# A diagonal state-space mixer worked through in batches of two group pairs

## The chip, the cores and the metric

The kernel runs on one core of a Trainium2 chip. The metric is the device time of one execution in microseconds (us), the median over runs. Times inside the execution come from one profiled execution and count from the start of its span. PE is the matmul engine, PEld its weight load, DVE the vector engine, ACT the scalar engine, POOL and SP the other two; SP issues nearly all DMA transfers.

## The reference

The program is one inference step of a two-layer streaming encoder on 1024 prompt positions and 64 sample positions, width 1024, all in fp32. Layer A mixes tokens with windowed attention, layer B with a complex-diagonal state-space model (S5); behind each mixer stands a gated convolutional FFN. The change lies in layer B's mixer alone. What it computes:

```
# 64 groups of 16 channels, a complex state of 64 numbers per group
x_t = B_bar u_t                        # per group, (64 x 16) complex
h_t = lambda_bar * h_(t-1) + x_t       # complex, elementwise, over positions
y_t = Re(C h_t) + d * u_t
z   = gelu(y)
ag  = z @ w_glu + b_glu
out = ag[:, :1024] * sigmoid(ag[:, 1024:])
```

## The kernel before

Activations lie with channels on partitions and the 1088 positions in three blocks of 384, 384 and 320 columns. Every large product is made of three fp32r products, of a high and a low half of both operands (`mm3`, L179); `load_unit` (L161) loads a 128 x 1024 piece of weight (tile `raw`, two buffers) and splits it into `whl` on ACT (L175) and DVE (L176). The program is attention, FFN 0, the state-space mixer `ssm`, its GLU, FFN 1.

The mixer. Eight positions form one column, so the scan runs over 137 columns (128 of the prompt, one empty, 8 of the sample). Two groups share the 128 partitions as a *pair* `q`, so there are 32 pairs. FFN 0 leaves the parameters of each pair in DRAM (`prm`, 1044 numbers per partition): input, direct and output matrices and a table of cosines and sines of the state's angle per column. Rotating by that angle makes the complex recurrence two real ones (real and imaginary part, `c` = 0, 1) with the decay `rho` that one DVE scan instruction (L979) runs over 2 x 138 columns. For each pair, `batch(q)` does

1. `ssm_pm`: load of the parameters (L926, SP) into `pm`, one of six `big` buffers; ACT copies the sines with a minus sign (L928) and writes the mask times rho (L929) beside them;
2. four input products on PE (L969) of `U`, the pair's input, into one of six PSUM banks; DVE multiplies by cosines and sines (L974, L975, the second reading the product's two halves in swapped order), adds (L976); POOL puts the sample's start state in (L977); then a `yield`;
3. DVE's scan (L979), two products to rotate back (L981, L982), ACT's copies of the last states (L985); a `yield`;
4. on PE a direct product of `U` (L990) and the state products (L995) into two PSUM banks, two ACT copies into `ys` (L999). After every fourth pair `ys` holds one tile of 128 channels with positions spread over partitions: it is written to DRAM (`yd`, L1002, ACT's queue), read back in the other arrangement (`yf`, L1007, SP), and ACT takes the gelu (`z`, L1012) and splits it into `zh` (L1019) and, with DVE, `zl` (L1020).

`staged` starts one pair a round and in each round advances the newest live pair first. `U` comes in four quarters of eight pairs (`ssm_load`, two transfers each from `hd`), and DVE multiplies each half quarter by the inverse norm `rs` (L919) as the load is written in the program. Within an engine the instructions run in a fixed order, which the builder's scheduler chose from readiness in its own timeline; SP's transfers stand in one queue.

The GLU (`tile_`, L1028) starts with the products of channel tiles 0 to 6 for its first 128 outputs, for the three blocks one after another, before it needs channel tile 7 (L1040, L1042).

Of the kernel before, what the change touches and what calls it, by code (L numbers as in the profile page):

```python
# [20 lines left out]
BLK = [(0, 384), (384, 384), (768, 320)]  # L21
# [9 lines left out]
NC_ = 137  # L31
NPR = 32

OW, OKT, OC, OCO, OSI, PRM = 0, 256, 512, 768, 906, 1044


class Core:
# [88 lines left out]
        return self.ps.tile([P, 512], F32, name=name, tag=f"sm{i}", bufs=1)  # L126

    @staticmethod
    def staged(units, beside=()):
# [779 lines left out]
    def ssm_load(self, q):  # L909

        nc = self.nc
        u = self.yp.tile([P, 16, NC_], F32, name="U", tag="ypB" if q == 2 else "ypA", bufs=1 if q == 2 else 2)
        for k in range(2):
            uk = u[:, 8 * k:8 * k + 8]
            self.last_u = nc.sync.dma_start(uk, self.hd[(2 * q + k) * P:(2 * q + k) * P + P].rearrange("(g j) s c -> (j s) g c", j=16))
            if k == 0:
                self.first_u = self.last_u
            for x, y in ((0, 2), (2, 8)) if (q, k) == (0, 0) else ((0, 8),):
                nc.vector.tensor_mul(uk[:, x:y], uk[:, x:y], self.rs[:, None, :].to_broadcast([P, y - x, NC_]))  # L919
        return u  # L920

    def ssm_pm(self, q):

        nc = self.nc
        pm = self.big([P, PRM + 414], "pm", F32)
        got = nc.sync.dma_start(pm[:, :PRM], self.prm[:, q])  # L926
        rd = pm[:, PRM + 138:].rearrange("p (c k) -> p c k", c=2)
        self.order(nc.scalar.activation(pm[:, PRM:PRM + 138], pm[:, OSI:PRM], AF.Copy, scale=-1.0), self.last_rs)  # L928
        self.order(nc.scalar.activation(rd, self.mask[:, None, :].to_broadcast([P, 2, 138]), AF.Copy, scale=self.rho[:, q:q + 1]), self.last_rs)  # L929
        return pm, pm[:, PRM + 138:], got  # L930

    def ssm(self, after):
        nc, tc, a = self.nc, self.tc, self.a
        off = PPO
        yd = self.dram.tile([D, 8, NC_], F32, name="yd")
        zh, zl = [None] * 3, [None] * 3
        with tc.tile_pool(name="ss", bufs=1) as sp:
            us = [self.ssm_load(0)]
            self.order(self.hw[1], self.first_u)
            self.order(self.hw[2], self.last_u)  # L940
            us.append(self.ssm_load(1))
            self.order(self.spill(), self.last_u)
            us.append(self.ssm_load(2))
# [5 lines left out]
            self.mask = sp.tile([P, 138], F32, name="mask")  # L949
            nc.gpsimd.memset(self.mask, 1.0)  # L950
            nc.gpsimd.memset(self.mask[:, 0:1], 0.0)
            nc.gpsimd.memset(self.mask[:, 129:130], 0.0)
            ROWS = (slice(0, 64), slice(64, 128))
            got, out = {}, {}

            def batch(q):
                if q == 8:
                    us.append(self.ssm_load(3))
                pm, rd, got[q] = self.ssm_pm(q)
                if q == 31:  # L960
                    self.wsrc.pop(0)
                    self.load_ahead(AHEAD)
                cos = pm[:, None, OCO:OSI].to_broadcast([P, 2, 138])
                sin = pm[:, OSI:OSI + 276].rearrange("p (c k) -> p c k", c=2)
                p1 = self.mm_ps("p1")[:, 0:2 * NC_].rearrange("p (c k) -> p c k", c=2)
                for c in range(2):
                    for e, r in enumerate(ROWS):
                        o = OW + P * c + 64 * e
                        nc.tensor.matmul(p1[r, c], pm[:, o:o + 64], U(2 * q + e), start=True, stop=True)  # L969

                wk = sp.tile([P, 3, 2, 138], F32, name="wk", bufs=5)
                A, t, G = (wk[:, i] for i in range(3))
                nc.gpsimd.memset(A[:, :, 0:1], 0.0)
                nc.vector.tensor_mul(A[:, :, 1:], cos[:, :, 1:], p1)  # L974
                nc.vector.tensor_mul(t[:, :, 1:], sin[:, :, 1:], self.from_last(p1))  # L975
                nc.vector.tensor_add(A[:, :, 1:], A[:, :, 1:], t[:, :, 1:])  # L976
                nc.gpsimd.tensor_copy(A[:, :, 129:130], h0[:, q, :, None])  # L977
                yield
                nc.vector.tensor_tensor_scan(G.rearrange("p c k -> p (c k)"), rd, A.rearrange("p c k -> p (c k)"), 0.0, ALU.mult, ALU.add)  # L979
                gc, gs = t, A  # L980
                nc.vector.tensor_mul(gc, G, cos)  # L981
                nc.vector.tensor_mul(self.from_last(gs), G, sin)  # L982
                for o, g_ in enumerate((gc, gs)):
                    x = g_[:, :, 128:138]
                    nc.scalar.copy(fin[:, o, q], bass.AP(tensor=x.tensor, offset=x.offset, ap=[x.ap[0], [138, 2], [9, 2]]))  # L985
                yield
                p3 = [self.mm_ps("p3")[:, :NC_] for _ in range(2)]
                for e in range(2):
                    o = OKT + P * e
                    nc.tensor.matmul(p3[e], pm[:, o:o + P], U(2 * q + e), start=True, stop=False)  # L990
                for c in range(2):
                    for g_ in (gc, gs):
                        for e, r in enumerate(ROWS):
                            o = OC + P * c
                            nc.tensor.matmul(p3[e], pm[r, o:o + P], g_[r, c, 0:NC_], start=False, stop=c == 1 and g_ is gs)  # L995
                if q % 4 == 0:
                    ys[0] = self.t4([P, 8, NC_], "ys")
                for e in range(2):
                    out[q] = nc.scalar.activation(ys[0][:, 2 * (q % 4) + e], p3[e], AF.Copy)  # L999
                if q % 4 == 3:  # L1000
                    kt = q // 4
                    nc.scalar.dma_start(yd[kt * P:kt * P + P].rearrange("(g i) t c -> (i t) g c", i=16), ys[0])  # L1002

                    for _ in range(min(6, 29 - q)):
                        yield
                    yf = self.t4([P, 8, NC_], "yf")
                    x = nc.sync.dma_start(yf, yd[kt * P:kt * P + P])  # L1007
                    if q < 28:
                        self.order(x, got[min(q + 8, 31)])
# [3 lines left out]
                    if q < 28:  # L1013
                        self.order(x, out[min(q + 5, max(out))])
                    nc.scalar.activation(z[:, SEQ:].rearrange("p (c t) -> p c t", t=8), yv[:, 129:137], AF.Gelu_apprx_tanh)
                    for b, (t0, n) in enumerate(BLK):
                        if kt == 0:
                            zh[b], zl[b] = self.bt(self.blk, b, "zh", F32R), self.bt(self.blk, b, "zl", F32R)
                        nc.scalar.activation(zh[b][:, kt], z[:, t0:t0 + n], AF.Copy)  # L1019
                        nc.vector.tensor_sub(zl[b][:, kt], z[:, t0:t0 + n], zh[b][:, kt].bitcast(F32))  # L1020
            self.staged([batch(q) for q in range(32)])
# [190 lines left out]
```

## Time and profile before

| | |
|---|---|
| runs | median 2365.73 us (2362.16 to 2365.94, 3 runs) |
| the profiled execution | 2358.86 us, its span 2357.1 us |
| PE busy | 2261.0 us (96%), weight loads 2190.1 us (93%) |
| DVE busy | 1469.9 us (62%) |
| ACT busy | 894.6 us (38%) |
| POOL busy | 278.9 us (12%) |
| granted TensorE clock, mean | 0.985 |

PE is busy for nearly all of the span except around 1200 to 1350 us. The profile's slices, 59 us each, show it:

```profile
PE   8999999999999999999957799999999999999997
DVE  8677639898576776564568722586555555465554
PEclk9999999999999999999978899999999999999998
```

Each digit is the busy share in tenths, and PEclk the granted clock in tenths. Slices 21 to 23, the norm ahead of the mixer and the mixer, are where PE is not full and the clock falls.

### The profile page before, as it was taken

How to read it: one execution, taken by the hardware profiler on the slowest of the kernel's cores; microseconds unless marked ns; L12 is line 12 of the kernel's file. 1: busy time of each engine (PE TensorE's matmuls, PEld its weight loads, DVE VectorE, ACT ScalarE, POOL GpSimd, SP SyncE). 2: the span in 40 equal slices, each digit the busy share in tenths (PEclk: the TensorE clock that was granted, in tenths of full speed). 3: DMA queues.
4: the chain of work that ended last, by engine and by line, in shares of the span. 5: the costliest groups of instructions: out<-in, count | busy, mean ns of one | idle time of the engine just before them, and what ended most of it. 6: DMA issues, size and time to landing. Idle time of an engine off the chain costs nothing. (4 is left out here: it accounts for less than half of the span.)

```text
span 2357.1 us, 35870 instructions
## 1 busy us (share of the span) xinstructions
PE 2261.0 (96%) x14265; PEld 2190.1 (93%) x14265; DVE 1469.9 (62%) x2892; ACT 894.6 (38%) x1487; POOL 278.9 (12%) x314
## 2 busy tenths in 40 slices
PE   8999999999999999999957799999999999999997
PEld 7987799999999999999955599999999999999997
DVE  8677639898576776564568722586555555465554
ACT  5256745322233334444535621343222222154332
POOL 5222006000122311020010000240000000000000
PEclk9999999999999999999978899999999999999998
DMA  5100015322344345664668621252222221165652
GB/s 188 34 29 19 28 50 176 117 69 103 93 135 137 126 147 156 222 214 148 193 233 246 186 87 37 72 157 86 80 78 74 84 74 64 53 211 181 211 178 94
DMA packets 167959, 287.02 MB, mean 122 GB/s; under 512 B 22032, under 2 KB 104496, under 8 KB 167664
## 3 DMA queue, kind: packets, MB, share of 16 engines
q1 hardware_dynamic: 157440, 273.41, 36.2%
q0 software_dynamic: 2032, 6.83, 0.9%
q10 hardware_dynamic: 8320, 4.49, 0.9%
q8 instruction: 112, 1.84, 0.3%
q14 instruction: 55, 0.45, 0.1%
HBM read 214.52 MB, written 70.17 MB: 121 GB/s over the span
## 5 line engine op out<-in xcount | busy, mean ns | idle before, releaser
L181 PE MATMUL mm<-hl,whl 128*128 128x384 f32 (+1 forms) x2232 | 733.5, 329 | 14.4 <-ACT whl L175 7.4
L183 PE MATMUL mm<-hh,whl 128*128 128x384 f32 (+1 forms) x2232 | 732.5, 329 | 1.8 <-DVE whl L176 1.8
L182 PE MATMUL mm<-hh,whl 128*128 128x384 f32 (+1 forms) x2232 | 733.6, 329 | 0.0
L175 ACT ACTIVATE whl<-raw 128x1024 fp32r<-128x1024 f32 x256 | 269.9, 1058 | 702.5 <-PE mm L183 576.9
L176 DVE TENSOR_TENSOR whl<-raw,whl 128x1024 fp32r<-128x1024 f32 x256 | 321.8, 1260 | 230.6 <-ACT whl L175 230.2
L181 PEld LDWEIGHTS mm<-hl,whl 128*128 128x128 f32 x2232 | 420.8, 189 | 16.1 <-DVE hl L247 8.5
L183 PEld LDWEIGHTS mm<-hh,whl 128*128 128x128 f32 x2232 | 420.5, 188 | 2.7 <-DVE whl L176 2.6
L182 PEld LDWEIGHTS mm<-hh,whl 128*128 128x128 f32 x2232 | 420.8, 189 | 0.4
L181 PE MATMUL mm<-gt,whl 128*128 128x384 f32 (+1 forms) x1056 | 344.6, 327 | 3.8 <-ACT y L392 3.0
L182 PE MATMUL mm<-gt,whl 128*128 128x384 f32 (+1 forms) x1056 | 343.9, 326 | 0.0
L183 PE MATMUL mm<-gt,whl 128*128 128x384 f32 (+1 forms) x1056 | 341.2, 326 | 0.7 <-DVE whl L176 0.7
L295 DVE TENSOR_TENSOR u<-rb,mm 128x384 f32<-128x384 f32 (+1 forms) x264 | 132.0, 507 | 280.0 <-PE mm L183 279.8
L181 PEld LDWEIGHTS mm<-gt,whl 128*128 128x128 f32 x1056 | 198.2, 188 | 4.9 <-ACT y L392 3.6
L183 PEld LDWEIGHTS mm<-gt,whl 128*128 128x128 f32 x1056 | 197.8, 188 | 1.0 <-DVE whl L176 1.0
L182 PEld LDWEIGHTS mm<-gt,whl 128*128 128x128 f32 x1056 | 198.2, 188 | 0.0
L303 ACT ACTIVATE t<-u,ppt 128x1090 f32<-128x1090 f32 x88 | 113.4, 1288 | 31.4 <-DVE u L297 19.8
L304 DVE SCALAR_TENSOR_TENSOR t<-u,ppt,t 128x1090 f32<-128x1090 f32 x88 | 118.9, 1352 | 8.3 <-ACT t L303 8.2
L305 DVE SCALAR_TENSOR_TENSOR t<-u,ppt,t 128x1090 f32<-128x1090 f32 x88 | 118.9, 1352 | 1.7
L266 POOL TENSOR_TENSOR y<-y,xl 128x768 f32<-128x768 f32 (+1 forms) x18 | 32.7, 1819 | 629.0 <-DVE y L264 486.7
L318 ACT ACTIVATE t<-t 128x1090 f32<-128x1090 f32 x44 | 49.0, 1114 | 102.2 <-DVE t L305 102.2
L1046 DVE SCALAR_TENSOR_TENSOR y<-pa,ppt,sg 128x384 f32<-128x384 f32 (+1 forms) x24 | 14.2, 593 | 95.7 <-ACT sg L1045 95.7
L370 DVE TENSOR_TENSOR gt<-gr,gt 128x768 fp32r<-128x768 f32 (+2 forms) x70 | 57.9, 865 | 18.5 <-ACT gt L369 18.5
(315 smaller groups left out, 3294.2 us busy)
## 6 DMA issues: line engine op xcount, KB each, us to landing
raw<-in_w_down SPq DMA_DIRECT2D x132, 512.0 KB, 4.0
raw<-in_w_up SPq DMA_DIRECT2D x88, 512.0 KB, 3.3
gd<-t SPq DMA_DIRECT2D x44, 512.0 KB, 2.6
pm<-prm SPq DMA_DIRECT2D x32, 522.0 KB, 5.4
gr<-gd SPq DMA_DIRECT2D x28, 384.0 KB, 4.7
xl<-x SPq DMA_DIRECT2D x24, 384.0 KB, 4.1
raw<-in_w_glu SPq DMA_DIRECT2D x16, 512.0 KB, 3.7
gr<-gd SPq DMA_DIRECT2D x22, 320.0 KB, 4.4
```

The source lines that it names most:

```text
L175: nc.scalar.activation(w[:, 0], raw, AF.Copy)
L176: nc.vector.tensor_sub(w[:, 1], raw, w[:, 0].bitcast(F32))
L181: nc.tensor.matmul(out, w[:, 0, sl], xl, start=start, stop=False)
L182: nc.tensor.matmul(out, w[:, 0, sl], xh, start=False, stop=False)
L183: self.last_mm = nc.tensor.matmul(out, w[:, 1, sl], xh, start=False, stop=stop)
L266: by[q].tensor_add(y[:, 2 * q:2 * q + 2], y[:, 2 * q:2 * q + 2], xs[q])
L295: nc.vector.tensor_mul(u[:, t0 + 2:t0 + 2 + np_], rb[:, t0:t0 + np_], ps[:, :np_])
L303: nc.scalar.activation(t, u[:, 0:T + 2], AF.Identity, bias=cb(m), scale=cw(0, m))
L304: nc.vector.scalar_tensor_tensor(t, u[:, 1:T + 3], cw(1, m), t, op0=ALU.mult, op1=ALU.add)
L305: nc.vector.scalar_tensor_tensor(t, u[:, 2:T + 4], cw(2, m), t, op0=ALU.mult, op1=ALU.add)
L318: nc.scalar.activation(ta, ta, AF.Gelu_apprx_tanh)
L370: nc.vector.tensor_sub(x[:, 1, j:j + e], raw, x[:, 0, j:j + e].bitcast(F32))
```

## The change

- `batch` takes two pairs at once (pairs 0, 1, 30 and 31 stay alone). Parameters of two pairs go to one `pm` tile (two transfers); input products still go pair by pair, now into the two single banks `sm0` and `sm1`; the two cosine and two sine multiplications ahead of the scan stay per pair, and the add, the scan (now 552 columns), and the two back-rotations become one instruction for two pairs.
- Both signs of the sines are copied to a tile `sc` of their own (in buffers of `raw`, later of `ypA`), and mask times rho to `rd` (two buffers); these ACT copies are ordered behind the last copies of final states (`turns`).
- POOL writes the start state ahead of the add instead of behind it.
- `staged` advances the oldest live batch first.
- The scaling of `U` is taken from the load and put in every fourth pair, ordered behind a scan; the third and fourth quarters are loaded later, and the third lies in a `big` buffer.
- `ys` goes to `yf` by eight SBUF to SBUF moves of 128 partitions to 16 each (L1032), without `yd`; at the end of the program text these moves' first one per tile is ordered behind a parameter load.

```diff
-            for v in list(reversed(live)):
+            for v in list(live if oldest else reversed(live)):
...
+                pm = self.big([P, 2, PRM], "pm", F32)
+                for e in range(2):
+                    got[t] = nc.sync.dma_start(pm[:, e], self.prm[:, 2 * t + e])
...
+                rd = sp.tile([P, 2, 2, 138], F32, name="rd", bufs=2)
...
+                for c in range(2):
+                    x = nc.scalar.activation(sc[:, :, c], pm[:, :, OSI:PRM], AF.Copy, scale=(1.0, -1.0)[c])
+                    self.order(x, turns[0])
+                for e, q in enumerate(qs):
+                    x = nc.scalar.activation(rd[:, e], mask[:, None, :].to_broadcast([P, 2, 138]), AF.Copy, scale=self.rho[:, q:q + 1])
+                    self.order(x, turns[0])
...
-                wk = sp.tile([P, 3, 2, 138], F32, name="wk", bufs=5)
+                wk = sp.tile([P, 2, n, 2, 138], F32, name="wk", bufs=3)
...
+                    p1[i] = self.sm_ps("p1", q % 2)[:, 0:2 * NC_].rearrange("p (c k) -> p c k", c=2)
...
+                    nc.vector.tensor_mul(A[:, i, :, 1:], cos[:, i, :, 1:], p1[i])
+
+                nc.gpsimd.tensor_copy(A[:, :, :, 129:130], h0[:, qs[0]:qs[0] + n, :, None])
+                for i in p1:
+                    nc.vector.tensor_mul(G[:, i, :, 1:], sc[:, i, :, 1:], self.from_last(p1[i]))
+                added = nc.vector.tensor_add(A[:, :, :, 1:], A[:, :, :, 1:], G[:, :, :, 1:])
...
+                scans.append(nc.vector.tensor_tensor_scan(flat(G), flat(rd), flat(A), 0.0, ALU.mult, ALU.add))
+
+                gc, gs = A, G
                 nc.vector.tensor_mul(gc, G, cos)
-                nc.vector.tensor_mul(self.from_last(gs), G, sin)
+                nc.vector.tensor_mul(gs, G, sc)
...
-                    nc.scalar.dma_start(yd[kt * P:kt * P + P].rearrange("(g i) t c -> (i t) g c", i=16), ys[0])
...
-                    x = nc.sync.dma_start(yf, yd[kt * P:kt * P + P])
...
+                    for g_ in range(8):
+                        x = nc.sync.dma_start(yf[16 * g_:16 * g_ + 16], ys[0][:, g_])
```

How the order of the engines moves. DVE, one pair in the middle of the mixer before (the names `p_` are the input products in PSUM):

```order
L974 TENSOR_TENSOR wk<-pm,p_11825 128x2x137
L975 TENSOR_TENSOR wk<-pm,p_11825 128x2x137
L976 TENSOR_TENSOR wk<-wk 128x2x137
L979 SCALAR_TENSOR_TENSOR wk<-pm,wk 128x276
L981 TENSOR_TENSOR wk<-wk,pm 128x276
L982 TENSOR_TENSOR wk<-wk,pm 128x2x138
```

DVE, one batch of two pairs in the middle of the mixer now, from the scan of one batch to the scan of the next:

```order
L1004 SCALAR_TENSOR_TENSOR wk<-rd,wk 128x552
L1007 TENSOR_TENSOR wk<-wk,pm 128x552
L986 TENSOR_TENSOR wk<-pm,p_12079 128x2x137
L986 TENSOR_TENSOR wk<-pm,p_12085 128x2x137
L1008 TENSOR_TENSOR wk<-wk,sc 128x552
L990 TENSOR_TENSOR wk<-sc,p_12079 128x2x137
L990 TENSOR_TENSOR wk<-sc,p_12085 128x2x137
L991 TENSOR_TENSOR wk<-wk 128x4x137
L1004 SCALAR_TENSOR_TENSOR wk<-rd,wk 128x552
```

Eight instructions stand for two pairs in place of twelve; the next batch's cosine products (L986) stand between the two back-rotations, its sine products (L990) behind them.

ACT at the same place before, with the sine copy (L928) of a later pair between the copies of one pair's last states (L985) and outputs (L999):

```order
L928 ACTIVATE pm<-pm 128x138
L985 COPY fin<-wk 128x4 x2
L999 ACTIVATE ys<-p_12041 128x137
L999 ACTIVATE ys<-p_12042 128x137
L929 ACTIVATE pm<-mask,rho 128x276
```

and now, for two batches (L1011 last states, L966 sines, L969 mask times rho, L1027 outputs, L1041 to L1048 gelu and split):

```order
L1011 COPY fin<-wk 128x8 x2
L966 ACTIVATE sc<-pm 128x2x138 x2
L969 ACTIVATE rd<-mask,rho 128x276 x2
L1027 ACTIVATE ys<-p_11955 128x137
L1027 ACTIVATE ys<-p_11956 128x137
L1027 ACTIVATE ys<-p_11970 128x137
L1027 ACTIVATE ys<-p_11971 128x137
L1041 ACTIVATE z<-yf 128x1024
L1043 ACTIVATE z<-yf 128x64
L1048 ACTIVATE zh<-z 128x384 x2
L1048 ACTIVATE zh<-z 128x320
L1011 COPY fin<-wk 128x8 x2
```

The sine copies of a batch now stand directly behind the last-state copies of the batch before it, and the gelu of a tile stands one batch behind the outputs that fill it.

SP's queue, a stretch in the first third of the mixer now, where before eight `pm` loads stood with two `yf` reads among them:

```order
L952 DMA pm<-prm 128x1044 x2
L1032 DMA yf<-ys 16x8x137 x7
L952 DMA pm<-prm 128x1044 x2
L1032 DMA yf<-ys 16x8x137
L952 DMA pm<-prm 128x1044 x2
```

The last move of a tile stands behind two parameter loads.

## Rows read from the trace of the kernel before

**Rows 1.** Busy time of the engines in stretches of the span (us from the span's start): start:end and length, then busy us and instructions of PE, PEld, DVE, ACT and POOL, the granted TensorE clock, the DMA engines' share and GB/s. The first stretch is the mixer of layer B, the second the start of the GLU behind it.
```profile
1221.00:1347.70 126.70, 92.88 (x896) 73.96 (x896) 105.55 (x220) 65.16 (x219) 9.43 (x60) 0.88 0.81 236
1347.70:1376.00 28.30, 25.30 (x149) 24.98 (x148) 9.32 (x15) 15.88 (x26) 0.00 (x0) 0.97 0.48 145
```

**Rows 2.** DVE's groups of instructions by line from 1218 to 1358 us: names, shapes, count; busy us and mean ns of one; idle time just before them and who ended it.
```profile
L979 DVE TENSOR_TENSOR_SCAN wk<-pm,wk 128x276 f32<-128x276 f32 x32 | 23.2, 731 | 7.7 <-POOL wk L973 6.8 <-POOL wk L977 0.8
...
L976 DVE TENSOR_TENSOR wk<-wk 128x274 f32<-128x274 f32 x32 | 14.1, 444 | 0.8
...
L919 DVE TENSOR_TENSOR U<-U,sel 128x1096 f32<-128x1096 f32 (+2 forms) x9 | 10.5, 1171 | 5.0 <-DMA U<-hd 3.1 <-ACT sel L907 1.8
L1020 DVE TENSOR_TENSOR zl<-z,zh 128x384 fp32r<-128x384 f32 (+1 forms) x21 | 10.1, 531 | 5.7 <-ACT zh L1019 5.6
L176 DVE TENSOR_TENSOR whl<-raw,whl 128x1024 fp32r<-128x1024 f32 x6 | 7.3, 1225 | 6.1 <-ACT whl L175 6.0
```

**Rows 3.** DVE's instructions in order of time over one pair's period (start us, duration us).
```profile
1246.60 0.45 DVE L981 TENSOR_TENSOR wk<-wk,pm 128x276 f32<-128x276 f32 x1
1246.96 0.44 DVE L982 TENSOR_TENSOR wk<-wk,pm 128x276 f32<-128x276 f32 x1
1247.32 0.43 DVE L974 TENSOR_TENSOR wk<-pm,p 128x274 f32<-128x274 f32 x1
1247.66 0.43 DVE L975 TENSOR_TENSOR wk<-pm,p 128x274 f32<-128x274 f32 x1
1248.13 0.45 DVE L976 TENSOR_TENSOR wk<-wk 128x274 f32<-128x274 f32 x1
1248.86 0.73 DVE L979 TENSOR_TENSOR_SCAN wk<-pm,wk 128x276 f32<-128x276 f32 x1 [0.28 <-POOL wk L973]
1249.63 0.45 DVE L981 TENSOR_TENSOR wk<-wk,pm 128x276 f32<-128x276 f32 x1
```

**Rows 4.** The U tile: the DVE instructions that scale it; duration ns as min/median/max, start of the first and the last, and the widths behind these durations.
```profile
L919 DVE TENSOR_TENSOR U<-U,sel x9: 445/1295/1302, 1221.0 to 1260.3; 128x1096 f32<-128x1096 f32 x7, 128x274 f32<-128x274 f32 x1, 128x822 f32<-128x822 f32 x1
```

**Rows 5.** ACT's instructions in order of time, from two places: the copies of the first pair's sine table (L928) and the mask times rho (L929), and a later final-state copy (L985) with the copy behind it.
```profile
1220.84 0.32 ACT L928 ACTIVATE pm<-pm 128x138 f32<-128x138 f32 x1
1221.05 0.53 ACT L929 ACTIVATE pm<-mask,rho 128x276 f32<-128x276 f32 x1
1221.46 0.32 ACT L928 ACTIVATE pm<-pm 128x138 f32<-128x138 f32 x1
...
1244.40 0.20 ACT L985 COPY fin<-wk 128x4 f32<-128x4 f32 x1 [0.16 <-DVE wk L982]
1244.50 0.31 ACT L928 ACTIVATE pm<-pm 128x138 f32<-128x138 f32 x1
...
1247.43 0.20 ACT L985 COPY fin<-wk 128x4 f32<-128x4 f32 x1 [0.16 <-DVE wk L982]
```

**Rows 6.** PE's instructions in order of time, two stretches: the first behind an idle time of 3.42 us, the second 17 us later. L969 is the input product of one pair, L990 the direct product and L995 the state product of one pair.
```profile
1271.04 1.28 PE L990 MATMUL p<-U,pm 128*128 128x137 f32 x4 [3.42 <-ACT ys L999]
1272.25 2.20 PE L995 MATMUL p<-wk,pm 64*128 64x137 f32 x16
1274.38 1.18 PE L969 MATMUL p<-U,pm 128*64 128x137 f32 x8
...
1290.77 0.69 PE L969 MATMUL p<-U,pm 128*64 128x137 f32 x8
1292.00 0.74 PE L990 MATMUL p<-U,pm 128*128 128x137 f32 x4 [0.54 <-ACT ys L999]
1292.67 1.20 PE L995 MATMUL p<-wk,pm 64*128 64x137 f32 x16
```

**Rows 7.** Stretches as in rows 1: behind that idle time, and the steady part of the mixer.
```profile
1271.00:1276.00 5.00, 4.96 (x30) 4.09 (x31) 4.33 (x11) 2.15 (x9) 0.44 (x4) 0.50 0.15 17
1290.00:1313.00 23.00, 16.38 (x192) 12.86 (x188) 19.71 (x44) 14.78 (x46) 1.32 (x12) 1.00 0.93 246
```

**Rows 8.** Transfers: an issue group of the whole program (count, KB each, median us to landing), the issue of eight such moves in a row with the ACT instruction that used them, and the time to landing of the eight yd<-ys writes (with the line of that tile's answer above it).
```profile
tl<-kd SPq DMA_DIRECT2D x64, 64.0 KB, 3.3
...
708.50 5.04 SPq L834 DMA_DIRECT2D tl<-kd  x8
...
718.54 2.02 ACT L835 ACTIVATE tp<-tl 128x1024 f32<-128x1024 f32 x1 [6.43 <-DMA tl<-kd]
...
L1002 ACTq DMA_DIRECT2D yd<-ys x8: 366/366/383, 1245.2 to 1355.9; - x8
...
DMA to landing us min/median/max: 3.3/6.2/9.6
```

**Rows 9.** Instructions in order of time at the end of the mixer: DVE's last L982, the GLU's first product on PE, the z of channel tile 6, its last zl, PE's next product, and then the z of channel tile 7 and the GLU's first sigmoid.
```profile
1345.44 0.44 DVE L982 TENSOR_TENSOR wk<-wk,pm 128x276 f32<-128x276 f32 x1
...
1347.71 0.69 PE L181 MATMUL pb<-zl,whl 128*128 128x384 f32 x1
...
1353.65 1.43 DVE L1020 TENSOR_TENSOR zl<-z,zh 128x384 fp32r<-128x384 f32 x3 [1.36 <-ACT zh L1019]
...
1354.26 0.45 PE L181 MATMUL pb<-zl,whl 128*128 128x384 f32 x1 [3.00 <-DVE zl L1020]
...
1367.93 2.15 ACT L1012 ACTIVATE z<-yf 128x1024 f32<-128x1024 f32 x1 [11.14 <-DMA yf<-yd]
...
1373.22 0.58 ACT L1045 ACTIVATE sg<-pb,ppt 128x384 f32<-128x384 f32 x1 [0.43 <-PE pb L183]
```

More of the change, by code (lines that the diff above doesn't have):

```diff
@@ L128, in staged @@
     @staticmethod
-    def staged(units, beside=()):
+    def staged(units, beside=(), oldest=False):
         live = []
@@ L948, in ssm @@
             ys = [None]
[L949 to L952, printed above, removed]
+            mask = sp.tile([P, 138], F32, name="mask")
+            nc.gpsimd.memset(mask, 1.0)
+            nc.gpsimd.memset(mask[:, 0:1], 0.0)
+            nc.gpsimd.memset(mask[:, 129:130], 0.0)
             ROWS = (slice(0, 64), slice(64, 128))
-            got, out = {}, {}
@@ L956, in batch, with params @@
[L956 to L960, printed above, removed]
+            tiles, got, turns, out = {}, {}, [self.last_rs], [None]
+            def params(t):
+                pm = self.big([P, 2, PRM], "pm", F32)
+                for e in range(2):
+                    got[t] = nc.sync.dma_start(pm[:, e], self.prm[:, 2 * t + e])
+                sc = self.wts.tile([P, D], F32, name="sc", tag="raw", bufs=2) if t < 8 else self.yp.tile([P, D], F32, name="sc", tag="ypA", bufs=2)
+                sc = sc[:, :552].rearrange("p (e c k) -> p e c k", e=2, c=2)
+                rd = sp.tile([P, 2, 2, 138], F32, name="rd", bufs=2)
+                tiles[t] = pm, sc, rd
@@ new lines, in batch @@
+            def batch(qs):
+                t, n, e0 = qs[0] // 2, len(qs), qs[0] % 2
+                if e0 == 0:
+                    params(t)
+                pm, sc, rd = tiles[t]
+                pm, sc, rd = (x[:, e0:e0 + n] for x in (pm, sc, rd))
+                for c in range(2):
[4 more added lines that the diff above has]
+                    self.order(x, turns[0])
+                if qs[-1] == 31:
@@ L971, in batch @@
-                wk = sp.tile([P, 3, 2, 138], F32, name="wk", bufs=5)
[L972 to L977, printed above, removed]
+                cos = pm[:, :, None, OCO:OSI].to_broadcast([P, n, 2, 138])
@@ new lines, in batch @@
+                nc.gpsimd.tensor_copy(A[:, :, :, 129:130], h0[:, qs[0]:qs[0] + n, :, None])
+                for i in p1:
+                    nc.vector.tensor_mul(G[:, i, :, 1:], sc[:, i, :, 1:], self.from_last(p1[i]))
+                added = nc.vector.tensor_add(A[:, :, :, 1:], A[:, :, :, 1:], G[:, :, :, 1:])
+                for q in qs:
+                    if q % 4 == 0 and q < 28:
+                        k = q // 4 + 1
+                        x = self.ssm_scale(us[k // 2], 8 * (k % 2), 8 * (k % 2) + 8)
+                        self.order(x, scans[-1] if scans else added)
@@ L986, in batch @@
+                turns[0] = x
                 yield
[L987 to L1001, printed above, removed]
-                    nc.scalar.dma_start(yd[kt * P:kt * P + P].rearrange("(g i) t c -> (i t) g c", i=16), ys[0])
-                    for _ in range(min(6, 29 - q)):
+                for i, q in enumerate(qs):
+                    p3 = [self.mm_ps("p3")[:, :NC_] for _ in range(2)]
+                    for e in range(2):
+                        o = OKT + P * e
+                        nc.tensor.matmul(p3[e], pm[:, i, o:o + P], U(2 * q + e), start=True, stop=False)
+                    for c in range(2):
+                        for s, g_ in enumerate((gc, gs)):
+                            for e, r in enumerate(ROWS):
+                                o = OC + P * (c ^ s)
+                                nc.tensor.matmul(p3[e], pm[r, i, o:o + P], g_[r, i, c, 0:NC_], start=False, stop=c == 1 and s == 1)
+                    if q % 4 == 0:
+                        ys[0] = self.t4([P, 8, NC_], "ys")
+                    for e in range(2):
+                        out[0] = nc.scalar.activation(ys[0][:, 2 * (q % 4) + e], p3[e], AF.Copy)
```

80 lines of the change are left out of this document (43 added, 37 removed).

## The prediction

> **What bounds the kernel now.** I read the stretches first. In the mixer, 1221.0 to 1347.7, DVE is busy for 105.55 of 126.7 us, PE for 92.88, ACT for 65.16 [rows 1]; nowhere else is PE left that idle, so what the mixer gains or loses passes to the end of the kernel: behind it PE works without a pause. That DVE is the bound, and not one busy engine among three, is seen in the order of time. In a stretch without other work DVE starts L981 at 1246.60 and again at 1249.63 [rows 3]: 3.03 us a pair, the only idle time in it 0.28 us behind POOL. Thirty-two such periods are 97.0 us. To these come the scaling of U, 10.5 us [rows 2], five of the tiles' zl splits (15 instructions; I take 0.45 us from start to start, below the mean of 0.531, since three in a row overlap: 6.8 us), three weight splits of 1.225 us (3.7): 118.0 us. From the first scaling at 1221.0 [rows 4] to the end of the last L982, 1345.44 + 0.44 = 1345.9 [rows 9], are 124.9 us. So 7 us are waits and everything else is DVE in a row. The last us ahead of the GLU are another matter: PE starts it at 1347.71, and stands for 3.00 us until 1354.26 because channel tile 6 is split only then [rows 9].
>
> **Fewer, wider DVE instructions.** Of the width I need the price of a double one. Scaling U takes 445 ns for 274 columns and 1295 ns for 1096 [rows 4]: 1.034 ns a column and a fixed 162 ns. A product or add over 552 (548) columns is then 0.73 us, where two of 0.444 were. From start to start it is less: independent instructions begin 0.09 us before their forerunner's end, dependent ones 0.03 behind it [rows 3]. For the scan there is one width, 276 columns in 731 ns [rows 2]. With the same fixed part it is 2.06 ns a column and 1.30 us for 552; if nothing of it is fixed, 1.46. I take 1.31, nearer the products' behaviour.
>
> Two pairs then cost, start to start: three products of 0.35 and one of 0.46 ahead of the dependent add, add 0.76, scan 1.34, two back-rotations of 0.65: 4.91 us, against 6.06. The 0.28 us behind POOL are in this: the start state is now written while DVE does the sine products. Fourteen batches are 68.7 us, the four single pairs at 0.35 + 0.46 + 0.47 + 0.76 + 0.72 = 2.76 another 11.0. Scaling stays 10.5. The order puts six tiles' zl (8.1) and four weight splits (4.9) ahead of the last L1008. Sum 103.2 us where 118.0 were: 14.8 less. If the scan is proportional, 2.2 less than that.
>
> **New waits on ACT.** Before, the sine copies ran pairs ahead. Now they stand on ACT behind the last-state copy of the batch before, which waits for L1008, and DVE's next sine product L990 waits for them. From rows: last-state copy 0.03 behind the DVE instruction, the next ACT instruction 0.10 later [rows 5], first sine copy 0.32 and second 0.43 (138 columns take 0.32 and the next starts 0.21 later; 276 columns of L929 begin 0.41 apart; two pairs' sines are 276 columns without L929's second operand), handing over 0.03: 0.9 us a batch. What stands on DVE between L1008 and L990 hides it. By the order now, four or five rounds have zl or weight splits there (1.35 or 1.23 us, hidden), the others nothing, or one or two cosine products of 0.35. I count some 6 us over fifteen rounds. At the start it is worse, since pair 0, pair 1 and batch 2-3 follow one another through this chain with nothing beside: three links, some 3 us. The first gelu, with its table load, holds zl back as before; 1.7 us. Together 10.7 us. Bounds: 4 if the scheduler's order fills more than I see, 17 if none of 17 links is hidden. Of the 7 us of waits before, those for U and zl are in these numbers; the others end.
>
> **PE.** Its work is the same: per pair 0.62 + 0.67 + 1.14, from the starts [rows 6], 4.9 us a batch at full clock. But the input products now have one bank each for even and odd pairs and stand behind the state products of the batch before. From L1008 to the next but one batch's L986, DVE has 0.9 + 0.8 + 0.76 + 1.34 + 0.65 = 4.45 us in a round without scaling; PE needs 2.3 for the state products and 1.2 for the input products, with the handovers 3.8: hidden. Behind a long idle time it is not: after 3.42 us without work the state product took 2.20 and the input product 1.18 us [rows 6], and the granted clock of that stretch was 0.50, the 1.2 GHz level, against 1.00 in 1290 to 1313 [rows 7]. Then PE needs some 6.3 us and DVE waits 1.9. In rounds with scaling and zl, 7.5 us long, PE idles for some 2.6 us, between the 2 us that left the clock alone and the 3.4 that did not. I take 3 us in all; bounds 0 and, with each of seven such rounds followed by one at half clock, 13.
>
> **Moving the outputs.** Eight moves of 68 KB replace a write and a read. The nearest rows are the `tl<-kd` loads, 64 KB to 16 partitions: 3.3 us to landing, and eight in a row, issued in 5.04 us, were used 10.0 us after the first issue [rows 8], so the last needed 5 us. A write to `yd` alone took 3.3 to 9.6. ACT takes z one batch (5.8 to 7.5 us) behind the last output: I cost the move at nothing, hidden by that batch; without this cover each late us stops ACT, and with it last states, sines and outputs. The Trainium skill ("DMA: Bandwidth & Descriptors", Rules for kernel authors) asks for the opposite, one large transfer in place of many small ones, and says that two transfers to disjoint partition halves serialize. If eight moves ran strictly one after another, at 3.3 us each they would need 26 us a tile, eight tiles 211 us where the mixer has 125, and the kernel 2445 us; the eight loads above took 10.0 us together, so the trace speaks against it, and I give it 1 in 100.
>
> Parameters now lie up to ten pairs ahead, not six, which ends ACT's waits for them; DVE never waited for these, so they count nothing. 64 issues of about 0.6 us [rows 8] in SP's 110 us stay beside the other work.
>
> **The end.** Tile 6 was behind by two hops and two rounds. Now it is split right behind the last L1008 (one weight split and three zl, 2.6 us), while PE does the last state products (1.8 us) and the GLU's first 18 products. So the 3.00 us go; bounds 0 and 3.3. Tile 7 came at 1367.93 and its sigmoid at 1373.22 [rows 9], just when PE had done the rest; now it has room.
>
> **Sum.** 103.2 + 10.7 + 3 = 116.9 us where 124.9 were, and 3.0 at the end: 11 us less. The profiled execution becomes 2358.9 - 11 = 2348; its time lies 7 us under the median of the runs shown, 2365.7, which becomes 2355.
>
> **Rivals.**
> *The chain hides.* If ACT's copies cost 4 and PE never waits, 103.2 + 4 = 107, and with 3 at the end the gain is 21 us: 2345. For it: DVE has filled waits well so far; against it: the order ties each sine copy to L1008.
> *The chain takes it back.* Links unhidden (17), a proportional scan (2.2), half clock (7 or more): 0 to 5 us are left, 2361 to 2366. For it: eight instructions in strict order across three engines, with one bank per input product, where before five pairs had buffers; against it: zl and scaling stand in half of the gaps.
> *The moves come late: slower.* The last move of a tile stands in SP's queue behind two parameter loads of 522 KB. If moves land as slowly as the slowest `yd` write, 9.6 us, they are 9.6 - 5.8 = 3.8 us late for z, seven times 27 us, less the 11: 2382. It turns slower at 1.6 us late per tile. Against it: the 5 us of the eight loads, which had other loads beside them.
> *No effect.* If PE, not DVE, set the pace, DVE's saving would leave the time as it is; against it 92.88 busy us in 126.7.
>
> **How the numbers follow.** Forecast, 7 to 16 us gained: 0.52. Hiding: 0.12. Taken back: 0.20, of which half is still beyond 4.7 us, or 0.2%, about the least that a measurement of this kernel can tell from none. Late moves: 0.10, the strictly serial ones among them, most of it slower. No effect: 0.06. Faster 0.75, same 0.16, slower 0.09. The range runs from hiding, 2345 less a us, to where the chain takes nearly all, 2364; it leaves out the late moves and the tails.
>
> **What would show it.** Right: DVE's batch period near 5.8 us in rounds without scaling and 7.5 in those with it; L1004 near 1.31 us and the wide products near 0.73; L990 waiting for L966 for 0.5 to 0.9 us in about half of the batches; the last L1008 near 1338; no wait for zl on PE at the GLU. Wrong: z waiting for yf in most tiles; L986 waiting for PE all through; a granted clock near 0.5 in most of the mixer, which would make PE the bound.

## The result, and the profile after

The changed kernel takes 2367.76 us, median of 20 runs, where the kernel before took 2362.34 in 20 runs beside it: 1.0026 of it, 95% interval 1.0018 to 1.0033, or 6 us more. The forecast was 11 us less, with 2344 to 2364 as the range.

The profiled execution took 2367.1 us (span 2365.3), 8.2 us more than that of before. 3.7 of them lie between the first scaling of U and the GLU's first sigmoid: 155.9 us (1222.08 to 1377.99) where 152.2 were (1220.99 [rows 4] to 1373.22 [rows 9]). 1.1 stand ahead of the mixer, 3.4 behind the sigmoid, of which the last section speaks.

The two stretches of [rows 1], the second a little longer:

```profile
1221.00:1347.70 126.70, 90.12 (x840) 75.06 (x839) 95.48 (x156) 64.11 (x186) 8.32 (x33) 0.80 0.75 229
1347.70:1377.00 29.30, 28.22 (x188) 26.92 (x186) 11.74 (x21) 14.11 (x32) 1.90 (x2) 0.89 0.35 103
```

DVE does 10 us less in the mixer's time of before, as meant, and no other engine took its place: PE and ACT are a little less busy as well. Everything waits more. PE's clock is granted at 0.80 where it was 0.88.

DVE's costliest groups from 1221 to 1360 us, shapes apart (columns as in [rows 2]):

```profile
L1004 DVE TENSOR_TENSOR_SCAN wk<-rd,wk 128x552 f32<-128x552 f32 x14 | 18.3, 1307 | 1.1
L986 DVE TENSOR_TENSOR wk<-pm,p 128x274 f32<-128x274 f32 x32 | 13.2, 433 | 4.1 <-DMA hd<-xs 2.2 <-PE p L985 1.5 <-issue 0.5
L990 DVE TENSOR_TENSOR wk<-sc,p 128x274 f32<-128x274 f32 x32 | 13.0, 436 | 11.8 <-ACT sc L966 11.8
L991 DVE TENSOR_TENSOR wk<-wk 128x548 f32<-128x548 f32 x14 | 10.2, 730 | 1.5
...
L1049 DVE TENSOR_TENSOR zl<-z,zh 128x384 fp32r<-128x384 f32 x14 | 7.4, 554 | 12.3 <-ACT zh L1048 12.3
```

The widths cost what was reckoned (1.307 and 0.730 us). The right-hand column is what is new: 12.3 us at zl, 11.8 at the sine product, 4.1 at the cosine product, 28 us in all. From the first scaling to the end of the last L1008 (1355.96) the mixer takes 133.9 us, where 124.9 were and 116.9 were forecast.

One undisturbed batch, in DVE's order of time (start, duration):

```profile
1299.27 1.31 DVE L1004 TENSOR_TENSOR_SCAN wk<-rd,wk 128x552 f32<-128x552 f32 x1
1300.61 0.73 DVE L1007 TENSOR_TENSOR wk<-wk,pm 128x552 f32<-128x552 f32 x1
1301.26 0.78 DVE L986 TENSOR_TENSOR wk<-pm,p 128x274 f32<-128x274 f32 x2
1301.96 0.73 DVE L1008 TENSOR_TENSOR wk<-wk,sc 128x552 f32<-128x552 f32 x1
1303.61 0.79 DVE L990 TENSOR_TENSOR wk<-sc,p 128x274 f32<-128x274 f32 x2 [0.93 <-ACT sc L966]
1304.51 0.73 DVE L991 TENSOR_TENSOR wk<-wk 128x548 f32<-128x548 f32 x1
1305.34 1.31 DVE L1004 TENSOR_TENSOR_SCAN wk<-rd,wk 128x552 f32<-128x552 f32 x1
```

6.07 us from scan to scan, for the two 3.03 us of [rows 3]: 5.14 without the wait of 0.93. A batch with nothing beside it thus wins nothing as long as the sine copies (L966) come last.

And the worst place. First ACT, then the DVE instructions on both sides of its longest wait, then SP's issues, and the time to landing of the one move issued from 1257.0 to 1258.5:

```profile
1256.39 0.92 ACT L969 ACTIVATE rd<-mask,rho 128x276 f32<-128x276 f32 x2
1264.59 1.28 ACT L1041 ACT_TABLE_LOAD   x1 [7.28 <-DMA pm<-prm]
1265.89 2.03 ACT L1041 ACTIVATE z<-yf 128x1024 f32<-128x1024 f32 x1
...
1260.35 0.73 DVE L1008 TENSOR_TENSOR wk<-wk,sc 128x552 f32<-128x552 f32 x1
1269.01 0.56 DVE L1049 TENSOR_TENSOR zl<-z,zh 128x384 fp32r<-128x384 f32 x1 [7.92 <-ACT zh L1048]
...
1251.99 2.15 SPq L1032 DMA_DIRECT2D yf<-ys  x2
1254.25 1.03 SPq L952 DMA_DIRECT2D pm<-prm  x2
1255.34 2.54 SPq L1032 DMA_DIRECT2D yf<-ys  x3
...
yf<-ys SPq DMA_DIRECT2D x1, 68.5 KB, 7.1
```

ACT comes to the first gelu at 1257.3 and stands there until 1264.6. The name beside the wait is a parameter load, but the gelu reads `yf`: its last move was issued by 1257.9, behind two such loads, and took 7.1 us to land. The DMA engines' share is 1.04 from 1240 to 1265. Behind the gelu on ACT stand output copies, last states and sine copies, and DVE's next instruction is that tile's zl, with the next cosine products behind it: both engines stop, and PE with them (7.4 us).

### The profile page after: what moved, and what is told of

The parts are those of the page before. It is cut to its first block, busy times and chain, and to the rows that moved or that the text cites. A ratio compares the mean times of both kernels' runs of the same rounds, so it can differ in the third digit from the quotient of the medians.

```text
span 2365.3 us, 35852 instructions
## 1 busy us (share of the span) xinstructions
PE 2269.7 (96%) x14265; PEld 2201.1 (93%) x14265; DVE 1463.6 (62%) x2836; ACT 893.6 (38%) x1463; POOL 282.1 (12%) x286
## 5 line engine op out<-in xcount | busy, mean ns | idle before, releaser
L1079 DVE SCALAR_TENSOR_TENSOR y<-pa,ppt,sg 128x384 f32<-128x384 f32 (+1 forms) x24 | 14.2, 594 | 99.6 <-ACT sg L1078 99.6
L1023 PE MATMUL p<-wk,pm 64*128 64x137 f32 x512 | 50.5, 351 | 23.3 <-DVE wk L1007 9.3
```

The lines of the kernel that those rows point to most:

```text
L1023: nc.tensor.matmul(p3[e], pm[r, i, o:o + P], g_[r, i, c, 0:NC_], start=False, stop=c == 1 and s == 1)
```

## The experiments

Differences below are ratios times 2362 us, so the changed kernel stands at +6.1 us. The intervals of two ratios leave a difference good to some 3 to 4 us, so that 3.3 and 3.8 us below stand at the edge of what these runs can tell. What was expected was partly written with medians, which differ from these by up to 3 us. "Gelu one round later" means one `yield` more between the moves and the gelu. The builder's scheduler chooses the order within the engines anew for every version, so an edit can shift other instructions too.

**First tile's gelu later.** One more condition behind the two `yield`s: 

```
                         yield
                         yield
+                    if kt == 0:
+                        yield
+                        yield
```

> The changed kernel with one difference: the gelu of the first channel tile (kt 0) stands two rounds later, all others where they are. Theory A (the first tile's moves land late, and the in-order ACT that waits for them stops DVE): the 7.9 us wait of DVE ahead of the first zl and most of the 4.2 us of the second tile's go, so 8 to 12 us less than the changed kernel, 0.997 to 0.999 of the kernel before. Theory B (the chain of last-state copy, sine copies and sine product sets the pace): the stop only hid waits that come anyway, under 2 us less, about 1.002. Theory C (the parameter loads of a saturated stretch set the pace there): DVE waits for PE's input products instead, which wait for pm; 0 to 4 us less, 1.001 to 1.0025.

Measured 1.0036 (1.0021 to 1.0051): no better than the changed kernel, and theory A had 8 to 12 us less. The profile shows a new wait (ACT, and DVE's longest):

```profile
1273.21 1.28 ACT L1043 ACT_TABLE_LOAD   x1 [6.88 <-DMA yf<-ys]
...
1277.51 0.79 DVE L990 TENSOR_TENSOR wk<-sc,p 128x274 f32<-128x274 f32 x2 [10.15 <-ACT sc L966]
```

The gelu now stands level with that of the second tile and waits for a move again, though its own tile's had long landed: the second tile's last move was issued at 1267.46 and took 5.6 us, to 1273.1. `ys`, `yf` and `z` share five buffers (`t4`); the likeliest reading is that `z` takes the buffer that these moves still read. No run shows this.

**Every gelu one round later.** For all tiles but the last:

```
                         yield
                         yield
+                        yield
```

> The changed kernel with the gelu of every channel tile but the last one round later (three rounds behind its outputs in place of two). Theory A: the first gelu would come near 1264 us, when its moves have just landed, and the later stops of 2.2 to 3.4 us on ACT go as well: 9 to 14 us less than the changed kernel, 0.996 to 0.9985 of the kernel before. Theory B: under 2 us less, about 1.002. Theory C: 0 to 4 us less.

Measured 0.9984 (0.9974 to 0.9993): 9.9 us less than the changed kernel, and below the kernel before. ACT's waits for moves up to 1356 us, first the changed kernel, then this one:

```profile
ACT L1041 <- DMA pm<-prm: 7.3, 1, 7.3
ACT z L1041 <- DMA yf<-ys: 6.2, 2, 3.4
...
ACT z L1041 <- DMA pm<-prm: 2.2, 1, 2.2
ACT z L1041 <- DMA raw<-in_w_glu: 2.2, 1, 2.2
```
```profile
ACT z L1041 <- DMA yf<-ys: 2.1, 1, 2.1
ACT L1041 <- DMA yf<-ys: 0.9, 1, 0.9
```

18 us of standing become 3. DVE's waits at zl up to 1350 us fall from 12.3 to 0.6, those at L990 from 11.8 to 6.7. Theory A holds for the row of tiles as a whole.

**Every gelu two rounds later.** A fourth:

```
                         yield
+                        yield
```

> The changed kernel with every gelu but the last two rounds later (four behind its outputs). With one round later ACT still stood 3.0 us for moves and DVE 6.9 us for zl. Theory A (late moves stop ACT): the rest goes too, 2 to 5 us less than with one round later, 0.996 to 0.998 of the kernel before. Theory that one round was enough: within 1.5 us of it, and if channel tile 6 is then late for the GLU, up to 3 us more.

Measured 1.0045 (1.0033 to 1.0058): 14 us worse than one round later. Now it is SP that waits:

```profile
SPq L1032 <- ACT zh L1049: 11.9, 2, 6.2
```

Moves into `yf` stand for the copies to `zh` of an earlier tile, behind which a `z` buffer comes free. The moves are late again by this, and ACT stands 16.6 us for them at four gelus. Of the three places that were run, one round later is the good one; on both sides of it long waits appear.

**Through DRAM.** Gelus one round later, and in place of the moves

```
+ nc.scalar.dma_start(yd[...], ys[0])
  yield; yield; yield
+ nc.sync.dma_start(yf, yd[...])
```

The reads of the first four tiles are tied behind a later parameter load.

> As the run with every gelu one round later, but the outputs go through DRAM as in the kernel before: one write a tile issued by ACT, one read on SP three rounds behind it, the gelu right behind the read. If the eight moves a tile are themselves the cost (64 issues in SP's queue, late landings), this is 3 us or more faster than that run. If the route is indifferent and only the place of the gelu counts, within 1.5 us of it. If the wait for write and read is what the direct moves save, it is slower by the read's 3 us or so wherever ACT comes to the gelu early, up to 10 us.

Measured 1.0037 (1.0023 to 1.0052), 12.5 us above the run with moves; but ACT stood 12.8 us in 4 for the read, which was issued right ahead of the gelu. The route itself was tried again below.

**The moves alone, in the kernel before.** 

```
-  nc.scalar.dma_start(yd[...], ys[0])
+  yf = self.t4([P, 8, NC_], "yf")
+  for g_ in range(8):
+      nc.sync.dma_start(yf[16 * g_:16 * g_ + 16], ys[0][:, g_])
   for _ in range(min(6, 29 - q)): yield
-  x = nc.sync.dma_start(yf, yd[...])
```

> The kernel before with the direct moves alone: eight moves from ys to yf where the write to DRAM stood, no read, the gelu six single rounds later as before; single pairs, newest first. If the moves cost nothing when the gelu is far behind: 0.999 to 1.000 of the kernel before, the lower end if the wait for channel tile 6 ahead of the GLU gets shorter. If 64 issues among the parameter loads delay these: 1.001 to 1.003.

Measured 1.0265 (1.0247 to 1.0282), 63 us more, far from both. Waits of SP and of ACT, 1222 to 1400 us:

```profile
SPq L1003 <- ACT ys L998: 95.7, 25, 5.5
```
```profile
ACT pm L928 <- DMA pm<-prm: 87.1, 21, 5.6
```

Without the tie that the change gives its moves (behind a parameter load), they stand early in SP's queue and wait there for outputs; the parameter loads behind them come late, ACT waits for these, and so do the outputs. With each move of pair q tied behind the load of pair q + 6:

> The kernel before with direct moves, each move of pair q tied behind the parameter load of pair q + 6, where the run with the moves alone had none. Theory that the 61 us of that run were SP's queue alone (96.8 us of SP standing ahead of moves whose outputs were not there, the parameter loads behind them): 0.999 to 1.002 of the kernel before. If the moves are dear by themselves: 1.005 or more still.

Measured 1.0033 (1.0021 to 1.0045). 55 of the 63 us were SP's order. The 8 that are left can't be put down to the moves: ACT waits 20.3 us for parameters where the kernel before has 14.4, the read's tie went with the read, and DVE now stands 2.40 us for the gelu of most tiles where it was 0.56.

**Sines untied.** For L966 and L969, so that these copies may run ahead:

```
-  self.order(x, turns[0])
+  self.order(x, self.last_rs)
```

With gelus one round later:

> Gelus one round later, and the sine and decay copies no longer tied behind the last-state copy of the batch before: they may run as soon as their parameters and a buffer are there. Theory B (this chain costs): the 6.7 us in 12 waits of L990 for L966, the three links at the start among them (0.69, 0.92, 0.58), go for the greater part: 4 to 7 us less than with one round later alone, 0.995 to 0.997 of the kernel before. If the two buffers of the sine tile or the banks of the input products hold DVE at the same places, 0 to 2 us less, 0.998.

Measured 0.9951 (0.9939 to 0.9964): 7.8 us less than with the gelus alone. Theory B holds beside A. L990 waits for L966 nowhere any more; DVE's waits move on (1215 to 1375 us):

```profile
DVE zl L1049 <- ACT zh L1048: 10.0, 4, 4.6
DVE wk L986 <- PE p L985: 7.8, 4, 2.4
DVE wk L986 <- PE p L1023: 3.2, 1, 3.2
```

The same edit on the changed kernel, gelus in place:

> The changed kernel with the sine and decay copies untied from the last-state copy, and the gelus where the change put them (two rounds behind). Gelus one round later gave 8.6 us and untied copies a further 8.7. If the two losses add up, this one gives 7 to 10 us of the changed kernel's loss back: 0.998 to 0.999 of the kernel before. If late moves hurt mostly because the sine copies stand behind the stopped gelu on ACT, it gives 12 to 16: 0.995 to 0.997.

Measured 1.0012 (1.0003 to 1.0022), 3.3 us less than the changed kernel: less than either expectation. The waits of DVE and of ACT, 1222 to 1350 us:

```profile
DVE zl L1049 <- ACT zh L1048: 22.6, 5, 12.7
```
```profile
ACT sc L966 <- DMA pm<-prm: 14.2, 5, 4.5
```

zl becomes DVE's wait, and the time that L990 gives back goes there. Late moves are only a part of it: ACT stands 7.1 us at four gelus, but 14.2 at the untied sine copies, which now come to parameters that haven't landed. In the longest wait at zl it stands 4.5 us at such a copy and then 3.6 at the gelu.

**Six banks for the input products.** First with gelus one round later, then with untied copies too:

```
-  p1[i] = self.sm_ps("p1", q % 2)[...]
+  p1[i] = self.mm_ps("p1")[...]
```

> Gelus one round later, and the input products in the six shared banks of the other products, as in the kernel before, in place of one bank each for even and odd pairs. If the single banks cost: the waits of L986 at the start (1.5 and 2.0 us) and a few tenths later go, 2 to 4 us less than with one round later alone, 0.997. If the six banks run short for the output products, 1 to 5 us more.

> Gelus one round later, copies untied, and the input products in the six shared banks. With the copies untied DVE waited 11.0 us at L986 for input products, where before that it had waited there for 4. If the single banks are what holds PE now: 3 to 8 us less than with both edits, 0.992 to 0.994 of the kernel before. If late parameter loads hold PE, or the six banks run short: 0 to 5 us more, 0.995 to 0.997.

Measured 1.0000 (0.9989 to 1.0010) and 0.9984 (0.9974 to 0.9994): 3.8 and 7.8 us worse than with one bank each. In the second run PE waits at its direct products (L1018) for ACT to empty a bank, 13.1 us in 8, where 4.4 in 5 stood without the edit: the shared banks run short. So going back to the shared banks wins nothing; what the single banks cost by themselves isn't shown, since the edit also takes two banks out of use.

**Moves issued by ACT.** In the changed kernel:

```
-  x = nc.sync.dma_start(yf[16 * g_:16 * g_ + 16], ys[0][:, g_])
+  nc.scalar.dma_start(yf[16 * g_:16 * g_ + 16], ys[0][:, g_])
```

> The changed kernel with its eight moves a tile issued by ACT, right behind the outputs, in place of SP, where parameter loads stand ahead of them. If the place in SP's queue makes them late: the gelus find their data, the 16 us of waits of DVE go, less what 64 issues cost ACT (the write to DRAM took ACT 0.37 us before): 5 to 10 us less than the changed kernel, 0.998 to 1.0005 of the kernel before. If the moves are late because they land slowly among the parameter loads: within 3 us of the changed kernel. If the issues stop ACT: 1.004 or more.

Measured 1.0051 (1.0039 to 1.0064). ACT's waits at the first seven gelus fall from 18 to 2.5 us, but each issue takes its time in ACT's queue:

```profile
L1032 ACTq DMA_DIRECT2D yf<-ys x64: 554/555/1359, 1239.1 to 1368.1; - x64
```

64 times 0.55 are 35 us of issuing on the engine that DVE waits for; some of it runs beside ACT's other instructions (the issue of 0.62 us at 1239.11 beside an L969 of 0.51 us at 1239.14). So ACT wins 15 us at the gelus and the kernel is 5.9 us slower. How much of the lateness was the place in SP's queue the run doesn't tell by itself. At the second tile ACT comes to the gelu at 1275.5, where the changed kernel has 1276.0, and doesn't wait. But at the first it comes 6 us later than in the changed kernel, and a move issued at 1256.0 took 9.6 us to land without any of SP's loads ahead of it in its queue.

**Through DRAM, with a round for the read.** Gelus one round later, untied copies:

```
+  nc.scalar.dma_start(yd[...], ys[0])
   yield; yield
+  nc.sync.dma_start(yf, yd[...])
   yield
```

> Gelus one round later, copies untied, and the outputs through DRAM: one write a tile on ACT's queue, the read on SP two rounds behind it and a round ahead of the gelu. If direct moves are worth something in this order of work: 4 to 12 us slower than the same kernel with direct moves, 0.997 to 1.000 of the kernel before. If the 11.7 us that the route through DRAM cost earlier came only from its read standing right ahead of the gelu: within 2 us of it, 0.995.

Measured 0.9984 (0.9969 to 1.0000): 7.8 us above the same kernel with direct moves. But at three of the first seven gelus ACT still stands for the read, where it stood at none of the seven with direct moves (1222 to 1350 us):

```profile
ACT z L1041 <- DMA yf<-yd: 8.8, 3, 3.8
```

So direct moves are the better route as both are placed here. A round trip with the time that it needs wasn't run.

**U later.** The third and fourth tile of U; first on the changed kernel, then with gelus one round later and untied copies, then with untied copies alone:

```
-  if qs[0] == 2:
+  if qs[0] == 6:
       us.append(self.ssm_load(2))
...
   if qs[0] == 4:
       self.order(self.spill(), self.last_u)
+  if qs[0] == 12:
       us.append(self.ssm_load(3))
```

> The changed kernel with the third and fourth tile of U asked for at batches 6 and 12 in place of 2 and 4: eight parameter loads, not four, go out ahead of the mixer, and fewer bytes stand in SP's queue and on the DMA engines from 1221 to 1265 us, where their share was 1.04 to 1.07. Theory that the first moves are late because of the load of that stretch: they land before the gelu, the 7.9 us stop of DVE and the 4.2 us behind it shrink, 6 to 12 us less than the changed kernel, 0.997 to 1.000 of the kernel before. Theory that a gelu two rounds behind is too early anyway: 0 to 4 us less, 1.001 to 1.0025.

> Gelus one round later, copies untied, and U asked for later. With the first two, ACT still stood 12.3 us in 6 for parameter loads and DVE 11.0 us for input products. If these come from the load of the first stretch: 4 to 9 us less than with the two edits, 0.991 to 0.9935 of the kernel before. If they come from the single banks and the clock of PE: within 2 us of it, 0.995.

> Copies untied and U asked for later, the gelus two rounds behind as the change has them. If one batch hides the moves when the first stretch is not overloaded, as the prediction had it: close to the kernel with all three edits, within 3 us, 0.991 to 0.996 of the kernel before. If the moves need a round more in any case: 6 us or more above it, 0.996 to 1.000.

Measured 1.0046 (1.0033 to 1.0059), 0.9929 (0.9917 to 0.9942) and 0.9982 (0.9972 to 0.9991). The load of the first stretch isn't the cause of the late moves: the DMA engines' share from 1240 to 1265 falls from 1.04 to 0.86, but ACT, which comes to the first gelu earlier, still waits 4.3 us, and then about 3 at each of the next four, 17.4 together where 18 were. And one batch of cover is too little with copies untied and U later as well: the third run lies 12.5 us above the second, which differs from it by the one `yield`. Why U later alone costs 4.7 us is open.

The second, with all three edits, takes 2346.47 us where the kernel before took 2362.94 beside it: 17 us less than the kernel before, and 23 less than the changed kernel. U later adds 5.2 us to the other two edits. ACT's waits at the sine copies, first without it, then with it:

```profile
ACT sc L966 <- DMA pm<-prm: 12.3, 6, 3.8
```
```profile
ACT sc L966 <- DMA pm<-prm: 4.3, 3, 1.7
```

DVE's waits for input products (L986, for PE) fall with them, from 11.0 to 4.1 us. The period of a batch is near the 5.8 us that were forecast, 5.67 here; but of the forecast 0.9 were the sine copies, which cost nothing now, and 0.42 here are a wait for PE:

```profile
1294.40 1.31 DVE L1005 TENSOR_TENSOR_SCAN wk<-rd,wk 128x552 f32<-128x552 f32 x1
...
1297.66 0.44 DVE L986 TENSOR_TENSOR wk<-pm,p 128x274 f32<-128x274 f32 x1 [0.42 <-PE p L985]
...
1300.07 1.31 DVE L1005 TENSOR_TENSOR_SCAN wk<-rd,wk 128x552 f32<-128x552 f32 x1
```

The edits together (ratio to the kernel before; the one empty place wasn't run):

| | copies tied | copies untied |
|---|---|---|
| gelu as changed, U early | 1.0026 | 1.0012 |
| gelu one round later, U early | 0.9984 | 0.9951 |
| gelu as changed, U later | 1.0046 | 0.9982 |
| gelu one round later, U later | | 0.9929 |

One `yield` is worth 9.9, 14.4 and 12.5 us in the three pairs, which the runs can hardly tell apart; untied copies 3.3, 7.8 and 15.1.

## Why the prediction was wrong

**The failing step: moving the outputs, "I cost the move at nothing, hidden by that batch".** It set a need of 5 us, the landing of the last of the eight loads, against a cover of 5.8 to 7.5, the time from the last output until ACT comes to the gelu. The third tile (kt 2), without the saturated start, shows both: ACT, SP, and the landing of the move issued at 1287.04.

```profile
1283.12 0.76 ACT L1027 ACTIVATE ys<-p 128x137 f32<-128x137 f32 x4
...
1290.07 0.46 ACT L1027 ACTIVATE ys<-p 128x137 f32<-128x137 f32 x2 [0.40 <-PE p L1023]
1292.72 2.04 ACT L1041 ACTIVATE z<-yf 128x1024 f32<-128x1024 f32 x1 [2.19 <-DMA raw<-in_w_glu]
...
1283.40 2.48 SPq L1032 DMA_DIRECT2D yf<-ys  x4
1285.98 1.00 SPq L952 DMA_DIRECT2D pm<-prm  x2
1287.04 0.55 SPq L1032 DMA_DIRECT2D yf<-ys  x1
...
yf<-ys SPq DMA_DIRECT2D x1, 68.5 KB, 5.4
```

The outputs are done at 1283.88 and ACT is at the gelu at 1290.53: 6.65 us of cover, as reckoned. The need is 8.6 us: 2.0 until four more moves are issued, 1.1 for two parameter loads that stand ahead of the last, 5.4 to land beside these loads. The landing is near the 5 that were set; what the term left out is the 3.1 us ahead of it, though the two loads in the queue were seen in the rival. So about 2 us are missing at this tile, where ACT waits 2.19, and 7.3 at the first, where landing took 7.1. ACT stands 18 us in five gelus; of this DVE gets 12.3 at zl and 4.2 at one L990: 16.5 us where the sum had 1.7.

The rival *moves come late* had the mechanism, its place in SP's queue and its turning point (1.6 us late per tile), at a chance of 1 in 10. Its price, 27 us, was too high: lateness is 7.3, 2.2, 2.2, 3.4 and 2.8, and nothing at two tiles, not 3.8 seven times; and it took the lateness from slow landing alone, not from the issues. The Trainium skill ("DMA: Bandwidth & Descriptors", Rules for kernel authors) asks for one large transfer in place of many small ones. No run here sets the two against each other on one route: eight moves were 7.8 us faster than one write and one read through DRAM, with ACT standing 8.8 us for that read.

**Fewer, wider instructions: right.** 1.307 us for the wide scan (1.31), 0.730 for the products (0.73), 5.14 us a batch without its wait, where 4.91 was the sum and 6.06 two pairs of before.

**New waits on ACT: right in size.** L990 waits 11.8 us, 4.2 of them behind the late second gelu; the 7.6 that are left stand against 9. The links at the start are 0.69, 0.92 and 0.58, and the others 0.20 to 0.93. Untying the copies gave 7.8 us with the gelus one round later.

**PE: near.** L986 waits 1.5 and 2.2 us at the start and 0.5 for an issue, and nowhere else: 4.2 where 3 stood. The second name, a load of `hd`, is hardly its cause: PE works without a pause from 1222.6 to 1228.8, with direct products ahead of the input products and an input product at first taking 1.18 us where it later takes 0.69 (granted 0.59 in the mean from 1221 to 1240, near the 1.2 GHz level).

**The sum.** 28.3 us of waits in place of 13.7. The moves alone make up this excess of 14.6: the waits put down to them are 16.5 where 1.7 stood. Work and handovers take 105.6 where 103.2 were set. Together 133.9 in place of 116.9.

**The end: right.** No product of the GLU waits for zl. Three rows, on DVE, PE and ACT:

```profile
1355.51 0.45 DVE L1008 TENSOR_TENSOR wk<-wk,sc 128x276 f32<-128x276 f32 x1
...
1354.88 0.44 PE L181 MATMUL pb<-zl,whl 128*128 128x384 f32 x1
...
1377.99 0.58 ACT L1078 ACTIVATE sg<-pb,ppt 128x384 f32<-128x384 f32 x1 [3.66 <-PE pb L183]
```

From the GLU's first product to its first sigmoid are 23.1 us where [rows 9] show 25.5: 2.4 of the 3.0 us. The GLU also starts earlier against the mixer, 1.08 us ahead of the end of the last L1008, where it started 1.83 behind the end of the last L982. So the 9.0 us that the mixer is longer come out as 3.7 at the sigmoid.

**Left over.** With the moves nearly on time (3 us of standing left) the same kernel gains 3.8 us, not 11. Its profile has the mixer up to the sigmoid 8.0 us shorter than before (1222.93 to 1367.20, 144.3 us). Some of the rest lies ahead of the mixer: the first scaling comes at 1221.5 to 1224.5 in all fourteen profiles of changed versions but at 1220.99 in that of before. Part of this can be the spread of single profiles, since the two versions of the kernel before with moves have 1222.96 and 1220.11. And some lies behind the first sigmoid: from there to the end the fourteen take 985.3 to 992.6 us, half of them up to 987.3, and the kernel before 983.9. Nothing that was run says why.

## What to carry to other kernels

When a DRAM round trip is replaced by direct moves, reckon from the last output to the last landing: issues one after another, what stands ahead of the last issue in its queue, and landing beside those very loads; then see how many buffers the delay holds, since a consumer put off too far stops the producer. An in-order engine that waits for a transfer stops everything queued behind it, so a microsecond late there costs three engines. And in a queue shared by loads and moves, a move must stand where its source is already done.

## What the runs showed beside

- Moves placed too early in SP's queue cost 55 us in a kernel whose DMA engines were busy for 0.81 of the mixer: 95.7 us of SP standing for outputs, with the parameter loads behind.
- Input products that share the six banks of the output products made the kernel slower than one bank each, by 3.8 and 7.8 us. The likeliest reading is that a product that may run ahead takes a bank that another's output needs.
- The same products of the FFN run at slightly different pace in two profiles. From the first sigmoid to the end are 983.9 us in the profile of before and 992.6 in that with gelus one round later, with `mm` products of 327 and 329 ns and a granted clock of 1.00 in all stretches but those at the joints. So the spans of two single profiles can differ by several us outside the mixer; the mixer's stretch alone, or many runs, settles smaller differences.
